# Moving operands of the attention half at 128 bytes past multiples of 256: a hybrid encoder layer on one core

## The chip, the core and the metric

The kernel runs on one core of one Trainium2 chip. The metric is the device time of one execution in microseconds (us). Before the change the median of three runs is 2173.73 us (2172.52 to 2175.91).

## What is computed

One layer of a streaming encoder, on 2048 prompt tokens and 64 sample tokens (2112 in all), width 1024, everything in float32. Cut to what matters:

```python
h = rmsnorm(x, g1) * (1 + sc1) + sh1
proj = h @ w_in                                  # 1024 -> 2568
u, q, k, v, o, gates = jnp.split(proj, cuts, -1)
pool_out = pool_mixer(u, ...)                    # four causal window means, each @ w_pool
hs = mlstm_seq(q, k, v, ig, lf, C, n, m)         # 4 heads of 128, chunks of 64
hs = normed(hs) * sigmoid(o)
x = x + gt1 * (concat([pool_out, hs], -1) @ w_out)
h2 = rmsnorm(x, g2) * (1 + sc2) + sh2
up = h2 @ w_up                                   # 1024 -> 5632
a, g = jnp.split(causal_conv3(up), 2, -1)
x = x + gt2 * ((silu(g) * a) @ w_down)           # 2816 -> 1024
y = rmsnorm(x, g_final)
```

The scales and shifts (sc, sh, gt) come from a conditioning vector through w_ada. The states of the mixers and of the convolution are outputs too.

## The kernel before

**Two halves.** Features lie on the 128 partitions, tokens along the free dimension. The attention half takes the tokens in four groups of 512 (the last one of 576, with the sample tokens), the feed-forward half in three groups of 704. TensorE works through them in a stream: for each group the V projection and the gates (lines 1069 and 1133), per head the projections of q, k and o, then four of u, then eight rows of the output projection. All projections but V go through `gemm` (line 468, its matmul is line 478).

**Three passes.** Every large product is made in float32r from a value split into a high and a low part: a tile has two rows of elements, `[P, 2, n]`, and each block of 128 weights is used three times, high x high, high x low, low x high (`PASSES`, line 463). So each matmul has a stationary operand of 128 x 128 out of a weight tile `wt` and a moving operand out of a tile of the activations:

```python
for pi, (a, b) in enumerate(PASSES):
    for bi, (lo, hi) in enumerate(o.blks):
        pe.matmul(ps[bi][:, :hi - lo], U[:, a, k % 4 * P:(k % 4 + 1) * P], mv[k][:, b, lo:hi],
                  start=(at == 0 and pi == 0), stop=(k == order[-1] and pi == 2))
```

`o.blks` is one block of 512 tokens in the first three groups, and blocks of 256 and 320 in the last. The moving operand `mv` is `hl` (the normed input, `hl_tile`, line 498) for q, k, o and u, and `mx` (the mixers' output, `mx_tile`, line 501) for the output projection. Both are tiles of 2 x 576 float32, 4608 bytes in a partition, so that the low part begins 2304 bytes, nine times 256, behind the high part. In the V projection `hl` is the stationary operand and `wt` moves.

**Weights.** They stream from HBM through SyncE's queue into `raw` buffers (five), and ScalarE and VectorE make high and low parts in `wt` (lines 411 and 414; seven buffers of 4352 bytes, 17 times 256). Weights that come a second time are loaded as split before. `pump` (line 421) keeps some units of work ahead of TensorE.

**Places in the partition.** Pools are stacks: one grows from the left, one from the right (line 93 on). On the left stand `cp` (constants), `wp` (`raw`, `wt`), then `hp` (`hl`), `sm`, `a1` and `a2` (the attention half's small tiles: q, k, th, at, kw, nd, the w4 buffers and others). On the right stand `sp` (scratch), a `gap` of 56 float32 (224 bytes) and `mx`. `half` (line 149) carries 32 float32 of filling, and so does each `wt` (line 175). The attention half's pools are given up before the feed-forward half (`leave`, line 1442), which puts its own tiles there: `hx` on the left, whose operands begin 32 float32 into a tile (`HO = 32`, line 46), and `av` on the right. In the feed-forward half line 1594 (`product`) moves `hx`, lines 2037 and 2160 move `av`; the weights are `wt` in each.

By the build, the operands' places are, in bytes past a multiple of 256:

| operand | where | before |
|---|---|---|
| wt, stationary | all products (moving in V) | 0 (V, 264 columns wide: 0, 32, 64, 96) |
| hl, moving | line 478; stationary in lines 1069, 1133 | 0 |
| mx, moving | line 478 | 0 |
| hx, moving | line 1594 | 128 |
| av, moving | lines 2037, 2160 | 160 or 32 |
| raw, five buffers | lines 411, 414 | 192, 0, 64, 128, 192 |
| q, k, th, at, kw, w4 | heads; line 857's loads | 128 |
| scr, ssum, rb | scratch | 224 |

In the attention half a scheduler orders the instructions of each engine by priority, in the feed-forward half and the first group the order is the program's.

Of the kernel before, what the change touches and what calls it, by code (L numbers as in the profile page):

```python
# [9 lines left out]
F32 = mybir.dt.float32  # L10
# [6 lines left out]
P = 128  # L17
# [47 lines left out]
def tile_layer(ctx: ExitStack, tc: tile.TileContext, xT, vecs, cst, rst, w_mod, w_ada, w_qkou, w_v, w_pool,  # L65
# [25 lines left out]
    rctx, actx = ExitStack(), ExitStack()  # L91
    fctx = ctx.enter_context(ExitStack())
    sp = rctx.enter_context(tc.tile_pool(name="sp", bufs=5, side="right"))
    gap = rctx.enter_context(tc.tile_pool(name="gap", bufs=1, side="right"))
    gap.tile([P, 56], F32, tag="gap", name="gap")
    mx = rctx.enter_context(tc.tile_pool(name="mx", bufs=KD, side="right"))
    hp = actx.enter_context(tc.tile_pool(name="hp", bufs=KD))
    sm = actx.enter_context(tc.tile_pool(name="sm", bufs=2))

# [2214 lines left out]
```

## Time and profile before

| | |
|---|---|
| profiled execution | 2174.68 us |
| its span, first to last instruction | 2172.9 us |
| granted TensorE clock, mean | 0.998 |
| matmuls, weight loads | 13553 each |
| attention half | to about 792 us of the span |
| HBM read, written | 410.98 MB, 125.98 MB |

The page of the profile gives, for each engine, busy time, share of the span and count; matmuls are pipelined, so that one begins while the one before it drains, and the mean duration of one is longer than the time from one start to the next (its period). Groups of instructions are given as line, engine, operation, tiles, size and count, then busy us and mean ns of one, then the idle time ahead of them and what ended it. The timeline merges like instructions in a row: start, length of the whole row, form and count. Waits are given as who waited for whom, total us, times, longest.

### The profile page before, as it was taken

What the parts mean: (1) busy time and instruction counts of PE and PEld (TensorE: products, weight loads), DVE (VectorE), ACT (ScalarE), POOL (GpSimd) and SP (SyncE); (2) the same over time, 40 slices, a digit from 0 to 9 for tenths busy, and PEclk for the clock granted to TensorE, in tenths of its full rate; (3) what the DMA queues carried; (4) which work ended last, traced back from release to release, by engine and by line L of the source; (5) the groups of instructions that cost most, each with busy time, mean ns of one, the idle gap of its engine ahead of it and who ended that gap; (6) DMA issues with size and microseconds to landing.
All of it is one profiled execution on the core that took longest, in us unless ns stands there. A gap on an engine that the chain in (4) does not pass through costs nothing.

```text
span 2172.9 us, 38060 instructions
## 1 busy us (share of the span) xinstructions
PE 2151.4 (99%) x13553; PEld 2044.4 (94%) x13553; DVE 1634.9 (75%) x3040; ACT 1096.1 (50%) x2181; POOL 258.4 (12%) x475
## 2 busy tenths in 40 slices
PE   8999999999999999999999999999999999999998
PEld 7888888888899999999999999999999999999998
DVE  5878668667955778797967668888886597887874
ACT  4554335334333446464736445655655365565554
POOL 0010000001000201010101220100101321111112
PEclk9999999999999999999999999999999999999999
DMA  8987997987888477888967976666668675555542
GB/s 319 328 305 233 323 321 246 309 302 244 301 283 288 169 260 239 282 292 300 350 214 255 321 245 222 234 208 209 228 222 274 223 255 186 170 177 190 171 160 77
DMA packets 297351, 539.51 MB, mean 248 GB/s; under 512 B 25760, under 2 KB 114336, under 8 KB 297160
## 3 DMA queue, kind: packets, MB, share of 16 engines
q1 hardware_dynamic: 286568, 511.87, 69.6%
q10 hardware_dynamic: 10592, 25.20, 3.0%
q8 instruction: 107, 1.75, 0.3%
q14 instruction: 84, 0.69, 0.1%
HBM read 410.98 MB, written 125.98 MB: 247 GB/s over the span
## 4 chain that ended last, share of the span: by engine, by line
PE 85%; DMA 5%; DVE 5%; issue 2%; ACT 2%; SPq 0%; POOL 0%; DVEq 0%; ACTq 0%; POOLq 0%
PE mm L1594 34%; PE mm L478 22%; PE mm L2160 12%; PE mm L2037 8%; PE mm L1133 3%; DVE wt L414 1%; DMA wt<-wsum 1%; PE m L1323 1%; DMA hl_kept<-wt 1%; PE m L1308 1%; PE m L1343 1%; PE m L1345 1%; DVE tg L1572 1%; DMA raw<-w_qkou 0%; ACT wt L411 0%
## 5 line engine op out<-in xcount | busy, mean ns | idle before, releaser
L1594 PE MATMUL mm<-hx,wt 128*128 128x352 f32 x5544 | 885.9, 321 | 0.7 <-DVE wt L414 0.5
L1594 PEld LDWEIGHTS mm<-hx,wt 128*128 128x128 f32 x5544 | 878.7, 188 | 2.6 <-DVE wt L414 2.0
L478 PE MATMUL mm<-hl,wt 128*128 128x512 f32 (+2 forms) x1920 | 387.4, 357 | 0.0
L411 ACT ACTIVATE wt<-raw 128x512 fp32r<-128x512 f32 (+3 forms) x470 | 276.6, 597 | 177.6 <-PE mm L478 52.8
L478 PEld LDWEIGHTS mm<-hl,wt 128*128 128x128 f32 x1920 | 316.4, 189 | 47.7 <-issue 4.4
L414 DVE TENSOR_TENSOR wt<-raw,wt 128x512 fp32r<-128x512 f32 (+3 forms) x470 | 312.8, 672 | 61.9 <-ACT wt L411 61.7
L2160 PE MATMUL mm<-av,wt 128*128 128x448 f32 (+1 forms) x1632 | 262.7, 322 | 0.0
L2160 PEld LDWEIGHTS mm<-av,wt 128*128 128x128 f32 x1632 | 250.4, 188 | 11.1
L2009 DVE SCALAR_TENSOR_TENSOR x<-mm,MOD,x 128x352 f32<-128x352 f32 (+3 forms) x360 | 167.5, 505 | 77.7 <-PE mm L2160 64.3
L2037 PE MATMUL mm<-av,wt 128*128 128x352 f32 x1344 | 220.7, 323 | 1.9 <-DVE x L2009 0.7
L2037 PEld LDWEIGHTS mm<-av,wt 128*128 128x128 f32 x1344 | 215.4, 188 | 5.0 <-DVE ea L1603 3.0
L1641 ACT ACTIVATE mm<-mm 128x352 f32<-128x352 f32 x196 | 87.8, 448 | 233.7 <-PE mm L1594 177.1
L478 PE MATMUL mm<-mx,wt 128*128 128x512 f32 (+1 forms) x960 | 182.9, 352 | 0.3 <-DVE scr L250 0.3
L478 PEld LDWEIGHTS mm<-mx,wt 128*128 128x128 f32 x960 | 159.4, 188 | 23.0 <-PE mm L478 0.5
L1572 DVE SCALAR_TENSOR_TENSOR ta<-ea,V,ta 128x704 f32<-128x704 f32 (+1 forms) x132 | 125.7, 953 | 58.4 <-ACT ta L1567 54.4
L1572 DVE SCALAR_TENSOR_TENSOR tg<-eg,V,tg 128x704 f32<-128x704 f32 (+1 forms) x132 | 125.7, 952 | 56.8 <-ACT tg L1567 54.3
L414 DVE TENSOR_TENSOR wt<-wt 128x512 fp32r<-128x512 f32 x196 | 133.0, 685 | 12.8 <-ACT wt L411 12.7
L411 ACT ACTIVATE wt<-wt 128x512 fp32r<-128x512 f32 x196 | 119.2, 622 | 36.6 <-DMA wt<-wsum 35.7
L1550 POOL COPY ea<-UC 128x2 f32<-128x2 f32 x66 | 33.1, 501 | 506.2 <-DVE ta L1572 407.3
L1781 ACT ACTIVATE tg<-tg 128x704 f32<-128x704 f32 (+1 forms) x66 | 52.5, 795 | 71.8 <-DVE tg L1572 71.8
L1133 PE MATMUL mm<-wt,hl 128*128 128x256 f32 (+1 forms) x576 | 71.4, 284 | 0.0
L1133 PEld LDWEIGHTS mm<-wt,hl 128*128 128x128 f32 x576 | 70.4, 190 | 0.8 <-issue 0.6
(305 smaller groups left out, 2207.0 us busy)
## 6 DMA issues: line engine op xcount, KB each, us to landing
wt<-wsplit SPq DMA_DIRECT2D x132, 512.0 KB, 4.3
raw<-w_up SPq DMA_DIRECT2D x198, 256.0 KB, 3.8
wt<-hl_kept SPq DMA_DIRECT2D x96, 512.0 KB, 6.3
wt<-wsum SPq DMA_DIRECT2D x132, 256.0 KB, 5.0
wsplit<-wt SPq DMA_DIRECT2D x66, 512.0 KB, 5.1
w<-w_up SPq DMA_DIRECT2D x88, 256.0 KB, 4.4
wsum<-w SPq DMA_DIRECT2D x44, 512.0 KB, 5.9
Bd<-fscr ACTq DMA_DIRECT2D x56, 352.0 KB, 4.3
```

Source lines behind the costliest of these rows:

```text
L411: act.activation(u.w[:, 0, :u.n], u.raw[:, :u.n], AF.Copy)
L414: dve.tensor_tensor(out=u.w[:, 1, :u.n], in0=u.raw[:, :u.n], in1=u.w[:, 0, :u.n].bitcast(F32), op=ALU.subtract)
L478: pe.matmul(ps[bi][:, :hi - lo], U[:, a, k % 4 * P:(k % 4 + 1) * P], mv[k][:, b, lo:hi], start=(at == 0 and pi == 0), stop=(k == order[-1] ...
L1133: pe.matmul(ps[ti][:n, :cols], h[4 * kh + k4][:, b, lo:lo + n], U[:, a, k4 % 2 * cols:(k4 % 2 + 1) * cols], start=(kh == 0 and k4 == 0 and ...
L1550: pool.tensor_copy(ext[:, 0:2], UC[:, f, :])
L1572: dve.scalar_tensor_tensor(out=t[:, :E], in0=ext[:, j:j + E], scalar=wc(j, f), in1=t[:, :E], op0=ALU.mult, op1=ALU.add)
L1594: pe.matmul(bk.t[:, :FH], U[:, a, kc * P:(kc + 1) * P], Bo.at(nm, kc, b), start=(first and kc == 0 and pi == 0), stop=(kc == 3 and pi == 2 ...
L1641: act.activation(to.t[:, :FH], bk.t[:, :FH], AF.Copy)
L1781: act.activation(self.tg[:, :E], self.tg[:, :E], AF.Silu)
L2009: dve.scalar_tensor_tensor(out=x3[n][:, a:b], in0=bk.t[:, a - lo:b - lo], scalar=gt2(n, s), in1=x3[n][:, a:b], op0=ALU.mult, op1=ALU.add)
L2037: pe.matmul(bk.t[:, :FH], U[:, a, c:c + P], quad.put(op, m, b), start=(first and m == 0 and pi == 0), stop=(m == 1 and pi == 2), skip_grou ...
L2160: pe.matmul(bks[i].t[:, :hi - lo], U[:, a, k % 4 * P:(k % 4 + 1) * P], av[k][:, b, lo:hi], start=(k == 0 and (a, b) == PASSES[0]), stop=(k ...
```

## The change

```diff
     sp = rctx.enter_context(tc.tile_pool(name="sp", bufs=5, side="right"))
     gap = rctx.enter_context(tc.tile_pool(name="gap", bufs=1, side="right"))
-    gap.tile([P, 56], F32, tag="gap", name="gap")
+    gap.tile([P, 24], F32, tag="gap", name="gap")
     mx = rctx.enter_context(tc.tile_pool(name="mx", bufs=KD, side="right"))
+    actx.enter_context(tc.tile_pool(name="hgap", bufs=1)).tile([P, 32], F32, tag="hgap", name="hgap")
     hp = actx.enter_context(tc.tile_pool(name="hp", bufs=KD))
     sm = actx.enter_context(tc.tile_pool(name="sm", bufs=2))
```

The gap on the right is 128 bytes smaller, so `mx` stands 128 bytes higher. A new unused tile of 128 bytes ahead of `hp` moves `hl` and all that lies behind it on the left by 128 bytes. After it `hl` and `mx` are at 128 past a multiple of 256; q, k, th, at, kw and w4 are on multiples; `wt`, `raw`, `scr` and every tile of the feed-forward half stay. The instructions, their order on each engine and their waits are the same in both programs; line numbers behind the change are one higher.

## The prediction

> **What bounds the kernel now.** I read the head of the page first, then its chain of waits, then the list of what TensorE waited for.
>
> ```profile
> span 2172.9 us, 38060 instructions
> PE 2151.4 (99%) x13553; PEld 2044.4 (94%) x13553; DVE 1634.9 (75%) x3040; ACT 1096.1 (50%) x2181; POOL 258.4 (12%) x475
> PE 85%; DMA 5%; DVE 5%; issue 2%; ACT 2%; SPq 0%; POOL 0%; DVEq 0%; ACTq 0%; POOLq 0%
> PE m L1032 <- DMA mx<-xT: 5.5, 1, 5.5
> PE m L1323 <- DVE kw L250: 1.9, 1, 1.9
> ```
>
> TensorE is busy for 99% of the span, 85% of the chain that ended last is its own, and its longest wait on another engine is 5.5 us at the start, its second longest 1.9 us. So the end is set by the sum of the matmuls' own periods, and a change that lengthens or shortens each of them by a nanosecond shows in full. The next view is busy time in stretches of the attention half (it ends at about 792 us).
>
> ```profile
> 60.00:150.00 90.00, 88.26 (x507) 74.73 (x506) 67.20 (x131) 48.55 (x121) 4.85 (x5) 1.00 0.93 338
> 225.00:380.00 155.00, 155.00 (x832) 131.18 (x831) 117.22 (x241) 62.28 (x149) 10.41 (x15) 1.00 0.87 296
> 560.00:615.00 55.00, 55.00 (x403) 51.99 (x402) 45.60 (x88) 17.11 (x34) 0.00 (x0) 1.00 0.90 300
> 60.00:792.00 732.00, 559.52 (x2836) 467.06 (x2834) 1.00 0.82 279
> ```
>
> The columns are the stretch, its length, busy time and instructions of PE, PEld, DVE, ACT and POOL, the granted clock, the DMA share and GB/s; the last row is the same for line 478 (the projections) alone. TensorE is full in each, at a granted clock of 1.00, so the throttle plays no part. The projections of line 478 are 559.5 of the 732 us: this is what the change can reach. The DMA share is 0.87 to 0.93, high but with no wait behind it.
>
> **The change part by part.** Both programs have the same instructions, waits and order on every engine; only addresses differ. What moves: the moving operands of line 478 (hl and mx, from 0 to 128 past a multiple of 256), hl as the stationary operand of the V projection (lines 1069 and 1133), and by the same 128 bytes all that lies behind hl (q, k, th, at, kw and the w4 buffers come from 128 onto multiples, others from one odd place to another). The weights wt stay on multiples of 256. Nothing is added that could wait; the only thing in question is how fast an unchanged instruction runs.
>
> First, how many there are, with the mean duration of one as the last number before the bar's idle part.
>
> ```profile
> L478 PE MATMUL mm<-hl,wt 128*128 128x512 f32 x1152 | 278.4, 396 | 0.0
> L478 PE MATMUL mm<-mx,wt 128*128 128x512 f32 x576 | 131.3, 389 | 0.0
> L478 PE MATMUL mm<-hl,wt 128*128 128x256 f32 x384 | 105.1, 287 | 0.0
> L478 PE MATMUL mm<-hl,wt 128*128 128x320 f32 x384 | 103.6, 311 | 0.0
> L478 PE MATMUL mm<-mx,wt 128*128 128x320 f32 x192 | 51.4, 312 | 0.3 <-DVE scr L250 0.3
> L478 PE MATMUL mm<-mx,wt 128*128 128x256 f32 x192 | 51.2, 281 | 0.0
> L1594 PE MATMUL mm<-hx,wt 128*128 128x352 f32 x5544 | 885.9, 321 | 0.7 <-DVE wt L414 0.5
> L2037 PE MATMUL mm<-av,wt 128*128 128x352 f32 x1344 | 220.7, 323 | 1.9 <-DVE x L2009 0.7 <-DVE wt L414 0.4 <-DVE ea L1603 0.3
> ```
>
> That is 1152 + 576 = 1728 matmuls of 512 columns and 2 x (384 + 192) = 1152 narrower ones, 2880 in all. Matmuls overlap, so these busy times aren't periods. For a period I take undisturbed stretches of the timeline: (length of the row minus one duration) / (count - 1).
>
> ```profile
> 157.52 11.18 PE L478 MATMUL mm<-hl,wt 128*128 128x512 f32 x48
> 347.02 25.36 PE L478 MATMUL mm<-mx,wt 128*128 128x512 f32 x111
> 766.83 18.45 PE L478 MATMUL mm<-mx,wt 128*128 128x320 f32 x137
> 793.85 11.16 PE L1594 MATMUL mm<-hx,wt 128*128 128x352 f32 x66
> 899.81 47.53 PE L1594 MATMUL mm<-hx,wt 128*128 128x352 f32 x298
> 1039.71 27.09 PE L1594 MATMUL mm<-hx,wt 128*128 128x352 f32 x170
> 1331.03 21.13 PE L2037 MATMUL mm<-av,wt 128*128 128x352 f32 x131
> ```
>
> Periods: hl 512: (11.18 - 0.396)/47 = 229.4 ns; mx 512: 24.97/110 = 227.0; the alternating 256 and 320 columns of the last group: (18.45 - 0.31)/136 = 133.4 for a mean of 288 columns; av 352: 20.81/130 = 160.1; hx 352: 47.21/297 = 159.0 and 26.77/169 = 158.4, but 10.84/65 = 166.8 in the row at 793.85. By the build, mx and hl lie on multiples of 256, av at 160 or 32 past one, hx at 128 past one, wt always on one.
>
> Two rows give a line: (227.0 - 160.1)/(512 - 352) = 0.418 ns a column, and 227.0 - 512 x 0.418 = 13.0 ns for each matmul besides. The third row fits it: 288 x 0.418 + 13.0 = 133.4. So operands at 0, 32 and 160 all pay 13.0 ns. Only hx, at 128, lies below the line, by 1.1 ns (159.0) to 1.7 ns (158.4). This is the one row of the trace in which a moving operand stands 128 bytes past a multiple of 256 against weights on one, which is what the change makes of line 478.
>
> *Term 1.* If the projections get hx's extra time: 2880 x 1.4 ns (the middle) = 4.0 us less; by the two ends 3.2 and 4.9.
> *Term 2.* The hl stretches run 2.4 ns above the mx stretches (229.4 against 227.0) at the same places. They are interrupted more often by the heads' matmuls, and take some time to settle afterwards. Whether the new place settles faster no row shows: between 0 and 1152 x 2.4 ns = 2.8 us; I take 1.0, near the lower end.
> *Term 3.* The V projection, 768 matmuls of 256 or 264 columns by the last four rows below (and a few on 64 weight columns). Here wt moves past hl, which becomes the operand at 128.
>
> ```profile
> 212.56 12.69 PE L1133 MATMUL mm<-wt,hl 128*128 128x264 f32 x103
> 602.38 1.53 PE L1133 MATMUL m<-wt,hl 128*64 128x256 f32 x12
> L1133 PE MATMUL mm<-wt,hl 128*128 128x256 f32 x288 | 36.0, 284 | 0.0
> L1133 PE MATMUL mm<-wt,hl 128*128 128x264 f32 x288 | 35.7, 284 | 0.0
> L1069 PE MATMUL mm<-wt,hl 128*128 128x264 f32 x96 | 14.1, 293 | 0.3 <-ACT hl L994 0.3
> L1069 PE MATMUL p<-wt,hl 128*128 128x256 f32 x96 | 12.1, 282 | 0.0
> ```
>
> Their period is (12.69 - 0.284)/102 = 121.6 ns; the line gives 120.0 for 256 and 123.4 for 264, a mean of 121.7. They sit on the line already, with wt at four different places for the 264. I take 0, with 768 x 1.4 ns = 1.1 us either way.
> *Term 4.* Other engines and DMA. The split of the weights reads its source from raw, whose five buffers stand at 192, 0, 64, 128 and 192 past a multiple of 256, or from wt on one:
>
> ```profile
> L411 ACT ACTIVATE wt<-raw 128x512 fp32r<-128x512 f32 x406 | 251.9, 622 | 139.0 <-PE mm L478 42.9 <-PE mm L2160 31.2 <-PE mm L2037 24.9
> L411 ACT ACTIVATE wt<-wt 128x512 fp32r<-128x512 f32 x196 | 119.2, 622 | 36.6 <-DMA wt<-wsum 35.7 <-DMA wt<-dsum 0.4
> raw<-w_up SPq DMA_DIRECT2D x198, 256.0 KB, 3.8
> wt<-wsum SPq DMA_DIRECT2D x132, 256.0 KB, 5.0
> w<-w_up SPq DMA_DIRECT2D x88, 256.0 KB, 4.4
> ```
>
> ScalarE takes 622 ns from either. A 256 KB load lands in 3.8 us at mixed places (raw), 4.4 at 128 (w) and 5.0 on multiples (wt): the order is not one of alignment. I cost both at nothing. TensorE at 99% hides them; if that cover went, the DMA share of 0.93 in the first group is what would come next, and the stretch 60 to 150 us would then keep none of its gain, about an eighth of term 1 (90 of 732 us), 0.5 us.
>
> Sum: -4.0 - 1.0 = -5.0 us. The profiled execution took 2174.7 us (its span of 2172.9 and 1.8 around it), 1.0 above the median of the runs; -5.0 on the median is 2168.7 us.
>
> A rule speaks against all of this. The Trainium skill, "TensorE: Matmul & The Clock Gate", Part 2, says that PE has two independent SBUF read ports and that loading the next weights takes no bandwidth from the running matmul; its section on the back-to-back gap gives N/2.4 + 2.5 ns. By it 512 columns would take an estimated 215.8 ns, and where the operands lie would not matter. The trace has 227.0 ns, and two periods (166.8 and 159.0) for one shape, so its second sentence does not hold here; the first I keep as a rival.
>
> **The rivals.** *Slower: the new place settles into a longer period.* The row at 793.85 shows 66 matmuls of the same line, shape and places as the 298 at 899.81, at 166.8 ns in place of 159.0: 6.7 ns above the line. So the address alone doesn't set the period; the phase in which a run of matmuls starts picks one of several steady patterns, and at 512 columns the pattern at 128 may be the long one. The hl stretches, 2.4 ns over the mx ones, are a milder form. Price: 1728 x 2.4 = 4.1 us to 1728 x 6.7 = 11.6 us, with the narrow ones as well 2880 x 6.7 = 19.3; its middle, 4.5 ns on 1728, is +7.8, or 2181.5 us. It decides from the point at which the extra time at 128 passes 13.0 ns a matmul. Against it: of 5544 matmuls at 128 only these 66 are shown so slow.
> *No change: 128 past is to the memory as good as on.* av at 160 and 32 differ by just 128 bytes and run in one stretch at one period of 160.1, and 0 fits the same line. For it too that the low period of hx may come from 352 columns and not from its place. It gives 2173.7 us. This is the case in which the skill's first sentence holds.
> *A larger gain.* The lowest fixed part in a row is that of 256 columns on 64 weight columns: (1.53 - 0.277)/11 = 113.9 ns, 6.1 below the line. 2880 x 6.1 = 17.6 us is the far end; half of it gives 2165.
>
> **How the numbers follow.** Forecast (terms 1 and 2; 2166 to 2172): 0.41. Slower pattern (2175 to 2193): 0.32. No change (2173 to 2175): 0.20. Larger gain (2156 to 2166): 0.07. A measurement of this kernel can tell about 0.2% from no change, which is 4.3 us: faster is below 2169.4, slower above 2178.1. Of the forecast about 0.31 lies below 2169.4 and 0.10 above, and of the slower rival 0.03 stays within the bound. Faster 0.38, same 0.33, slower 0.29. The range leaves out the far half of the larger gain and the slow pattern on all 2880 matmuls: 2162 to 2183. The likeliest case's own range is 2166 to 2172.
>
> **What would show it.** In the profile of the changed kernel the undisturbed mx stretch of 512 columns at about 347 us should have a period near 225.5 (forecast), 227.0 (no change) or 230 to 234 (slower); the mean duration of mx 512 should go from 389 to about 387.5, or stay, or rise by as much as the period. The pair rows of the last group should go from 133.4 to about 132. The first L1594 should start about 5 us earlier, and all from there on should be as before, since no operand of the feed-forward half moves; if its own stretches change, a phase that is carried over is at work, and the forecast would be wrong by a mechanism that I priced only for the attention half: a shift of 1 ns there is worth 5.5 us on line 1594 alone.

## The result and the profile after

The changed kernel takes 2179.89 us (median of 12 runs, 2175.75 to 2182.34); the kernel before took 2173.47 us in the same session (12 runs, 2170.73 to 2176.05). The ratio is 1.0028, with a 95% interval of 1.0020 to 1.0036: 4.3 to 7.8 us slower, middle 6.1. The forecast was 5.0 us faster. What came is the first rival, a longer settled period, at about three quarters of its price. The profiled execution took 2181.35 us (span 2179.6).

From the page of the changed kernel: head, chain of waits, and the list of what TensorE waited for. All line numbers are one higher than before.

```profile
span 2179.6 us, 38060 instructions
PE 2158.0 (99%) x13553; PEld 2044.9 (94%) x13553; DVE 1635.6 (75%) x3040; ACT 1095.0 (50%) x2181; POOL 257.7 (12%) x475
PE 89%; DVE 4%; DMA 3%; issue 1%; ACT 1%; SPq 1%; POOL 0%; ACTq 0%; DVEq 0%; POOLq 0%
PE m L1324 <- DVE kw L251: 2.3, 1, 2.3
PE m L1309 <- ACT at L251: 1.8, 1, 1.8
```

The counts are the same, and the added time is TensorE's own: its busy time went from 2151.4 to 2158.0 us (+6.6) for a span that grew by 6.7. VectorE, ScalarE and GpSimd stayed within 1.1 us. Of the waits, that of line 1309 grew most, from 0.5 to 1.8 us; that of line 1230 (1.5 us before) is gone. Next the groups of instructions by form, mean ns of one as the last number before the bar:

```profile
L479 PE MATMUL mm<-hl,wt 128*128 128x512 f32 x1152 | 283.0, 400 | 0.1
L479 PE MATMUL mm<-mx,wt 128*128 128x512 f32 x576 | 134.4, 395 | 0.0
L479 PE MATMUL mm<-hl,wt 128*128 128x320 f32 x384 | 103.2, 308 | 0.0
L479 PE MATMUL mm<-mx,wt 128*128 128x320 f32 x192 | 50.1, 303 | 0.3 <-DVE scr L251 0.3
L1595 PE MATMUL mm<-hx,wt 128*128 128x352 f32 x5544 | 884.9, 321 | 0.1
```

Two signs in one change: 512 columns went up (hl 396 to 400, mx 389 to 395 ns), 320 columns went down (311 to 308, 312 to 303). The feed-forward form of line 1595, which does not move, kept its 321. Periods come from the timeline's stretches, as in the prediction:

```profile
339.78 10.43 PE L479 MATMUL mm<-hl,wt 128*128 128x512 f32 x44
350.51 44.77 PE L479 MATMUL mm<-mx,wt 128*128 128x512 f32 x192
765.82 35.14 PE L479 MATMUL mm<-mx,wt 128*128 128x320 f32 x269
802.87 11.16 PE L1595 MATMUL mm<-hx,wt 128*128 128x352 f32 x66
```

mx 512: (44.77 - 0.395)/191 = 232.3 ns, where it was 227.0. hl 512: (10.43 - 0.400)/43 = 233.3, where a stretch had 229.4. The pairs of the last group: (35.14 - 0.31)/268 = 130.0, where they were 133.4. The last row repeats the odd stretch of 66 feed-forward matmuls to the digit, 11.16 us. In a later execution of the same changed kernel the same 66 matmuls took the short period, (10.61 - 0.321)/65 = 158.3 ns in place of 166.8:

```profile
798.32 10.61 PE L1595 MATMUL mm<-hx,wt 128*128 128x352 f32 x66
```

In the single starts of the trace, mx 512 before is 227, 227, 226 without end; after, it goes round in sevens (for example 228, 229, 233, 240, 234, 230, 232) and never comes to a constant. hl 512 before comes to the same 227, 227, 226, after about nine starts of 225 to 236 ns behind an interruption; in the stretch at 339.78 after, its starts alternate between 229 and 238.

Where the time went, as the length of each phase of the program (from the first matmul of a phase to the first of the next, in us; groups added up). Beside the first profile of each kernel stands the one of its later profiles that has no step, both taken in one session on one chip; "steps" are the drops of the granted clock in the attention half, of which more below.

| execution | V projection | hl 512 | mx 512 | last group, hl | last group, mx | feed-forward | steps | time |
|---|---|---|---|---|---|---|---|---|
| before | 109.97 | 344.52 | 130.78 | 136.33 | 51.70 | 1375.46 | 1 | 2174.68 |
| before, later | 110.52 | 342.85 | 130.78 | 135.55 | 52.07 | 1376.45 | 0 | 2174.50 |
| changed | 109.82 | 348.82 | 133.93 | 138.48 | 51.13 | 1372.88 | 2 | 2181.35 |
| changed, later | 109.54 | 347.63 | 133.95 | 133.58 | 52.82 | 1375.70 | 0 | 2179.33 |

Between the two executions without a step: hl 512 +4.8, mx 512 +3.2, V projection -1.0, last group -2.0 and +0.75, 5.6 us in all to the end of the attention half (with -0.1 at the start). The feed-forward half gives between 1372.9 and 1376.5 us in one or the other, in both directions. What the narrow forms give back also differs between executions of one program: the mx pairs of the changed kernel run at 130.0 ns in three of its four profiles, and in the fourth ("changed, later") at the old (38.52 - 0.31)/286 = 133.6:

```profile
757.89 38.52 PE L479 MATMUL mm<-mx,wt 128*128 128x320 f32 x287 [0.29 <-DVE scr L251]
```

### The profile page after: what moved, and what is told of

It is laid out like the page before. It is cut to its first block, busy times and chain, and to the rows that moved or that the text cites. A ratio compares the mean times of both kernels' runs of the same rounds, so it can differ in the third digit from the quotient of the medians.

```text
span 2179.6 us, 38060 instructions
## 1 busy us (share of the span) xinstructions
PE 2158.0 (99%) x13553; PEld 2044.9 (94%) x13553; DVE 1635.6 (75%) x3040; ACT 1095.0 (50%) x2181; POOL 257.7 (12%) x475
## 4 chain that ended last, share of the span: by engine, by line
PE 89%; DVE 4%; DMA 3%; issue 1%; ACT 1%; SPq 1%; POOL 0%; ACTq 0%; DVEq 0%; POOLq 0%
PE mm L1595 37%; PE mm L479 23%; PE mm L2161 12%; PE mm L2038 8%; PE mm L1134 3%; DVE wt L415 1%; PE m L1324 1%; PE m L1309 1%; PE m L1346 1%; PE m L1344 1%; DMA raw<-w_ada 1%; DVE tg L1573 0%; PE mm L1070 0%; ACT tg L1568 0%; DVE x L2010 0%
## 5 line engine op out<-in xcount | busy, mean ns | idle before, releaser
L479 PE MATMUL mm<-hl,wt 128*128 128x512 f32 (+2 forms) x1920 | 392.0, 360 | 0.1
L415 DVE TENSOR_TENSOR wt<-wt 128x512 fp32r<-128x512 f32 x196 | 133.3, 686 | 10.6 <-ACT wt L412 10.6
```

What stands on the lines that cost most here:

```text
L415: dve.tensor_tensor(out=u.w[:, 1, :u.n], in0=u.raw[:, :u.n], in1=u.w[:, 0, :u.n].bitcast(F32), op=ALU.subtract)
```

## The experiments

**Which tile: hl, mx, or what moved along.** Three variants of the kernel before, each with a part of the change. `agap` is one more unused tile, behind `hp`; with it, 256 bytes in all put the small tiles back on their old residues.

```diff
 hl only:
+    actx.enter_context(tc.tile_pool(name="hgap", bufs=1)).tile([P, 32], F32, tag="hgap", name="hgap")
     hp = actx.enter_context(tc.tile_pool(name="hp", bufs=KD))
+    actx.enter_context(tc.tile_pool(name="agap", bufs=1)).tile([P, 32], F32, tag="agap", name="agap")
 mx only:
-    gap.tile([P, 56], F32, tag="gap", name="gap")
+    gap.tile([P, 24], F32, tag="gap", name="gap")
 small tiles only:
     hp = actx.enter_context(tc.tile_pool(name="hp", bufs=KD))
+    actx.enter_context(tc.tile_pool(name="agap", bufs=1)).tile([P, 32], F32, tag="agap", name="agap")
```

> hl alone stands 128 past a multiple of 256; mx and the small tiles behind hl stay where they were. Theory (the residue of the moving operand against that of the weights sets the period at which a run of matmuls settles): the hl matmuls of 512 columns at about 237 ns as in the changed kernel, mx 512 at 227.0, the hl pairs of 256 and 320 columns about 7 ns a pair shorter than before; 2.5 to 5 us slower than before (2176 to 2179 us). Rival (the tiles that moved along with hl, or their DMAs, are the cause): about 2173.5, with hl 512 at 233.5.

> mx alone stands 128 past a multiple of 256. Theory: mx 512 at 232 in place of 227 ns, 576 x 5 = 2.9 us more, less 192 pairs x 7 ns = 1.3 us; about 1.5 us slower (2175), hl as before. Rival (small tiles): no change and mx 512 at 227.

> hl and mx stay on multiples of 256; only what lies behind hl (q, k, th, at, w4 and so on) moves by 128 bytes as in the changed kernel. Theory: no change (2172.5 to 2174.5), periods as before. Rival (small tiles): slower by up to 6 us.

Measured, against the kernel before on the same chip (2173.08 us): hl only 2175.39, ratio 1.0009 (1.0000 to 1.0018); mx only 2174.52, 1.0006 (0.9998 to 1.0015); small tiles only 2172.13, 0.9994 (0.9986 to 1.0003). The times alone hardly part them, the phases do: mx 512 takes 133.94 us with mx moved and 130.71 and 130.78 in the other two; hl 512 takes 345.82 with hl moved and 342.52 and 342.34 in the other two (no clock step in any of the three). The timeline's mx stretch of the kernel before and of two of them:

before:
```profile
347.02 43.72 PE L478 MATMUL mm<-mx,wt 128*128 128x512 f32 x192
```
mx only:
```profile
347.81 44.77 PE L478 MATMUL mm<-mx,wt 128*128 128x512 f32 x192
```
small tiles only:
```profile
346.61 43.72 PE L479 MATMUL mm<-mx,wt 128*128 128x512 f32 x192
```

With mx alone moved, the stretch has the changed kernel's 44.77 us to the digit. The rival that tiles or DMAs behind hl make the loss falls. "hl only" came out just under what was expected (2175.4 against 2176 to 2179), and the shorter pairs expected of it do not show: its hl part of the last group took 135.88 us, against 135.01 and 135.51 in the other two.

**Against what does the place count?** If the residue of hl and mx by itself mattered, moving the weights would do nothing; if the place relative to the weights matters, moving both restores the old time and moving the weights alone gives the new one. The pad behind an early tile shifts wt by 128 bytes, and with it all that lies behind it on the left: raw, hl and the small tiles. So when all are to move, the unused tile ahead of `hp` falls away and the gap of 24 stays; when wt alone is to move, that tile stands there as in the changed kernel, which brings hl and the small tiles back to their old residues, and the gap is 56 as before.

```diff
-    half = cp.tile([P, 8 + 32], F32, tag="half", name="half")[:, :8]
+    half = cp.tile([P, 8 + 64], F32, tag="half", name="half")[:, :8]
```

> As the changed kernel, with the weights wt moved by 128 bytes as well, so that hl and mx stand at 0 relative to the weights, but at 128 absolutely. If the place relative to the weights decides: hl and mx 512 at 227 to 234 as before, about 2173.5 us for the attention half (the feed-forward half changes too: hx would stand at 128 relative as before, since it moves along). If the absolute residue of the moving operand decides: 232 ns for mx 512 as in the changed kernel, about 2180.

> The weights wt alone move by 128 bytes; hl, mx and the small tiles stay where they were. Theory of the relative place: the projections run as in the changed kernel (mx 512 at 232 ns, pairs at 260), 2176 to 2182 us. Theory of the absolute place of hl and mx: mx 512 at 227.0 as before, 2173.5 us.

The mx stretch with hl, mx and wt all moved:
```profile
346.31 43.72 PE L478 MATMUL mm<-mx,wt 128*128 128x512 f32 x192
```
The same with wt alone moved:
```profile
351.05 44.96 PE L479 MATMUL mm<-mx,wt 128*128 128x512 f32 x192
```

All moved: 43.72 us, as before. Weights alone: 44.96 us, hl 512 at 349.34, the time 2181.45 against 2174.53 us, ratio 1.0035 (1.0024 to 1.0047), although neither hl nor mx was touched (some 2.4 us of it belong to the feed-forward half, as the next paragraph shows). So it is the distance of the moving operand from the stationary one, modulo 256 bytes, that decides, and not an alignment of either. The Trainium skill, "TensorE: Matmul & The Clock Gate", Part 2, has two independent SBUF read ports, one for the streaming operand and one for the weights; these two runs speak against their being independent here.

The kernel with all three moved did not come back to 2173: 2175.95 us, ratio 1.0023 (1.0012 to 1.0033). Its attention half did (hl 512 341.90, mx 512 130.81), but moving wt changes the feed-forward half's distances to av, which stays. By form, before and with all moved:

```profile
L2160 PE MATMUL mm<-av,wt 128*128 128x448 f32 x816 | 178.8, 363 | 0.0
L2160 PE MATMUL mm<-av,wt 128*128 128x256 f32 x816 | 111.0, 280 | 0.0
```
```profile
L2160 PE MATMUL mm<-av,wt 128*128 128x448 f32 x816 | 181.8, 367 | 0.0
L2160 PE MATMUL mm<-av,wt 128*128 128x256 f32 x816 | 110.4, 279 | 0.0
```

The means go from 363 to 367 and from 280 to 279 ns: 816 x (4 - 1) = 2.4 us. Five of its 12 runs lie at 2180.8 to 2184.1 us, apart from the rest; their mean granted clock is 0.997 or 0.998, that of the others 0.997 to 0.999. The profile shows an execution of 2172.83, so what those five had is open.

**TensorE alone.** Next the cost by itself: no other engine and no DMA at work, rows of 72 matmuls with the weights on a multiple of 256 and the moving operand at each of eight places.

```python
    for blks in FORMS:
        for r in PLACES:
            t = [mv[r, k] for k in range(2)]
            for rep in range(2):
                run([small, small], ((0, 132),), 4 + 3 * rep, 0)
                last = run(t, blks, 72 // len(blks), r // 4)
```

> Leaves the computation out: TensorE alone runs unbroken rows of 72 matmuls of one form each (512, 448, 352, 256, 264 columns, and the pairs 256+320 and 288+288), the weights on a multiple of 256 and the moving operand 0, 32, 64 ... 224 bytes past one, each twice from different starting phases; ScalarE, VectorE and the DMA queues stand still meanwhile. Theory (matmul and weight load meet in the memory, and the place of the one against the other sets where a row settles): 512 columns at 0 settle at 226.7 ns, at 128 at 231 to 234; 352 columns at 128 at 158 to 159; the pair 256+320 at 267 for 0 and 260 for 128; the 256 and 264 columns differ by under 2 ns. Rival (the other engines' and the DMAs' traffic make the difference in the kernel): no difference between the places here, all at one line.

Its timeline, the second row of four places (the operand's name has the place in bytes):

```profile
132.68 16.55 PE L100 MATMUL mm<-by0b,wt 128*128 128x512 f32 x72
201.56 16.71 PE L100 MATMUL mm<-by64b,wt 128*128 128x512 f32 x72
270.84 16.95 PE L100 MATMUL mm<-by128b,wt 128*128 128x512 f32 x72
305.67 17.08 PE L100 MATMUL mm<-by160b,wt 128*128 128x512 f32 x72
```

A row has one longer matmul at its start. Without the first six the trace's starts give, for each place in bytes:

| columns | 0 | 32 | 64 | 96 | 128 | 160 | 192 | 224 |
|---|---|---|---|---|---|---|---|---|
| 512 | 226.7 | 233.3 | 228.9 | 233.4 | 232.3 | 234.3 | 233.3 | 233.4 |
| 352 | 160.0, 161.2 | 160.0 | 160.0 | 162.2 | 158.4, 166.7 | 160.0 | 160.0 | 160.1 |
| 256 and 320, mean | 133.1 | 130.9, 131.6 | 131.4 | 133.3 | 133.1 | 132.0 | 131.5 | 133.6 |

(The first row of all, 512 at 0, began at half the clock and is left out of the table.) The kernel's 227.0 and 232.3 ns come back without its traffic, so the rival of the other engines' and the DMAs' share falls. At 512 columns place 0 is the best of the eight; the kernel before stood on it. Where a cell has two numbers, the two starting phases settled differently. The pairs at 128 missed the expectation: 133.1 from both phases here, 130 in the changed kernel. So did the 256 and 264 columns, which were to differ by under 2 ns: they range from 116.7 to 120.0 and from 120.0 to 126.7 by place. And place 0 is not the best for every width: 448 columns take 202.7 ns there and 200.0 at 64.

**The starting phase.** Rows of the same kind, each form eight times behind three matmuls of eight different widths.

> Leaves the computation out, as m_place: rows of 72 matmuls, each form and place eight times, with eight different widths of the three matmuls ahead of it and so eight starting phases. Theory (place, column count and starting phase together pick the settled period): 512 at 0 always at 226.7, 512 at 128 at 232.3 or longer every time, 352 at 128 at 158.4 from some phases and 166.7 from others, 352 at 0 at 160 to 161, pairs at 0 always near 266, at 64 near 263, at 128 at 260, 266 or 271 depending on the phase. Rival (the place alone decides): one period for each form and place.

Four of its 56 rows, 352 columns at 128 and at 0:

```profile
444.10 11.72 PE L101 MATMUL mm<-by0b,wt 128*128 128x352 f32 x72
467.79 11.62 PE L101 MATMUL mm<-by128b,wt 128*128 128x352 f32 x72
479.53 12.20 PE L101 MATMUL mm<-by128b,wt 128*128 128x352 f32 x72
491.85 11.61 PE L101 MATMUL mm<-by128b,wt 128*128 128x352 f32 x72
```

352 at 128 settles at 158.3 to 158.4 ns from six phases and at 166.7 from two; at 0 it is 160.0 from all eight. 512 at 0: 226.7 to 227.0 (one row 228.9, the first, begun at half the clock); 512 at 128: 232.3 to 232.5 from six, 233.4 from two, never less. The pairs: 133.1 at 0 and 131.4 or 131.5 at 64 from all, 129.8 or 133.1 at 128, four times each (271 ns a pair was not seen). The place alone does not set the period; place, column count and the way the row begins do. What was varied is the width of the matmuls ahead; that it acts through the starting phase is the reading of it. In the whole kernel even the same program gives either period, as the two executions of the 66 matmuls above show.

**A better version?** The pairs gain where the 512 columns lose, so the last group alone was moved. hl and mx lie at 64 (or 128), and the first three groups use them from column 48 (or 32) on, which puts their operands back at 0.

```diff
+        o.sh = 0 if o.last else 48
...
-            d = hl_tile(k)
+            d = hl_tile(k)[:, :, o.sh:]
...
-            mix[:NH] = [mx_tile(gi) for gi in range(NH)]
+            mix[:NH] = [mx_tile(gi)[:, :, o.sh:] for gi in range(NH)]
```

> hl and mx lie 64 past a multiple of 256, and the first three groups use them from column 48 on, so that their 512-column operands stand at 0 as before; only the last group's pairs and its V projection stand at 64. By the rows of the kernel in which TensorE ran alone (pairs 131.4 a matmul at 64 against 133.1 at 0, from either starting phase): mx 512 at 227.0 as before, the pairs at 262.8 in place of 267, 576 x 4.2 = 2.4 us less than before, about 2170.5. If the last group then waits longer for the heads' chain on ScalarE and VectorE, part of this is lost.

> The same with the last group at 128 past, as in the changed kernel, and the first three groups at 0 (their column 32 on). If the changed kernel's 260 ns a pair hold: 576 x 7 = 4 us less than before, 2169; if the pairs at 128 settle at 266 to 271, as in the kernel in which TensorE ran alone and in the kernel with the weights moved, no gain to 2 us more.

A third way leaves all addresses and cuts the last group at column 288:

```diff
-        o.blks = [(0, 256), (256, 576)] if o.last else [(0, GT)]
+        o.blks = [(0, 288), (288, 576)] if o.last else [(0, GT)]
```

> Everything lies where it lay before; only the last group is cut at column 288 in place of 256 (two blocks of 288 in place of 256 and 320), so that its second block starts 128 past a multiple of 256 and the first on one. Theory: the pairs lie between 260 ns (both blocks at 128) and 267 (both at 0), so 576 pairs x 0 to 7 ns, 0 to 4 us less than before: 2169.5 to 2173.5. Rival (only the column counts matter): 2 x (288 x 0.418 + 13.0) = 266.8 a pair, no change.

None can be told from the kernel before: at 64, 2174.26 us against 2175.35, ratio 0.9995 (0.9986 to 1.0005); at 128, 2173.96, 0.9998 (0.9989 to 1.0006); cut at 288, 2172.82 against 2174.53, 0.9992 (0.9983 to 1.0002). The last stretch of mx pairs, with the place at 64 and then at 128:

```profile
756.24 38.04 PE L481 MATMUL mm<-mx,wt 128*128 128x320 f32 x287 [0.29 <-DVE scr L252]
```
```profile
752.35 38.52 PE L481 MATMUL mm<-mx,wt 128*128 128x320 f32 x287 [0.29 <-DVE scr L252]
```

The cut at 288 also agrees with TensorE alone, where the two blocks of 288 take 133.2 ns a matmul at place 0, as 256 and 320 do (133.1). At 64 the pairs run nearly as TensorE alone said (131.4), (38.04 - 0.31)/286 = 131.9 a matmul. At 128 they fell into the other pattern, 133.6. With the place at 64 TensorE also stands 1.6 us for line 1311 and 1.1 us once for VectorE's scr:

```profile
PE m L1311 <- ACT at L252: 1.6, 1, 1.6
PE mm L481 <- DVE scr L252: 1.4, 2, 1.1
```

That waiting took the gain is not shown: at the first of the two waits (its line 1308) the unchanged kernel itself stood 0.5, 1.6 and 0.3 us in its three profiles. Nor is it shown that there was no gain, since the interval at 64, from 3.0 us faster to 1.1 slower, holds the 2.4 us expected.

**The clock steps.** The changed kernel's profile shows a granted clock below 1.00 in two places, at the waits of lines 1324 and 1309:

```profile
430.00:450.00 20.00, 17.65 (x90) 14.86 (x89) 11.59 (x27) 4.23 (x11) 1.01 (x1) 0.91 0.92 327
690.00:700.00 10.00, 8.21 (x39) 7.09 (x37) 5.46 (x13) 3.89 (x11) 0.00 (x0) 0.66 1.00 330
```

Whether such a step follows from idle time was asked of TensorE alone: 72 rows of 512 columns at place 0, with nine lengths of idle time between them.

```python
            for _ in range(n):
                dve.tensor_tensor(out=tmp, in0=tmp, in1=tmp, op=ALU.max)
            dve.scalar_tensor_tensor(out=t[0][:, 0, :128], in0=tmp, scalar=0.0, in1=src[:, :128], op0=ALU.mult, op1=ALU.add)
            last = run(t, ((0, 512),), 60 + rep, 0)
```

> Leaves the computation out: TensorE alone runs 72 rows of 60 to 67 matmuls of 512 columns at place 0, and between two rows stands idle for nine different times (about 0.8 to 3.5 us), each eight times, because the next row's operand is written by a chain of VectorE instructions behind the row before. Theory (an idle time of about 2 us makes the clock step down in some executions, which is the part of the changed kernel's loss that varies): no half-clock matmuls (427 ns) after gaps under 1.5 us, after gaps of 1.8 to 2.5 us in some of the eight, after 3 us and more in most; a step costs 2 to 5 us. Rival (the steps in the kernels have another cause): no half-clock matmuls after any gap here, or no relation to its length.

Its timeline, first round (the idle time ahead of a row stands in brackets):

```profile
129.24 13.90 PE L98 MATMUL mm<-by0b,wt 128*128 128x512 f32 x60 [1.03 <-DVE by0b L113]
160.23 13.84 PE L98 MATMUL mm<-by0b,wt 128*128 128x512 f32 x60 [1.78 <-DVE by0b L113]
176.18 15.45 PE L98 MATMUL mm<-by0b,wt 128*128 128x512 f32 x60 [2.10 <-DVE by0b L113]
212.31 16.71 PE L98 MATMUL mm<-by0b,wt 128*128 128x512 f32 x60 [2.76 <-DVE by0b L113]
250.95 13.84 PE L98 MATMUL mm<-by0b,wt 128*128 128x512 f32 x60 [3.42 <-DVE by0b L113]
```

60 matmuls take 13.84 us without a step, 15.45 or 16.71 with one. After idle times of 0.8 to 1.8 us none of 32 rows had one; after 2.1 to 3.4 us 21 of 40 had, and not even 3.4 us brings it every time. A step costs 1.5 to 1.7 us (18 rows, 7 or 8 starts of 427 ns) or 2.7 to 2.9 us (three rows, 13 such starts), where 2 to 5 were expected. The Trainium skill, "TensorE: Matmul & The Clock Gate", Part 1, gives an idle window of about 3.4 us that runs freely and does not begin with the idle time. That one idle time has a step and the next of the same length has none agrees with a free window, and so do the lengths in the traces, where the granted clock holds one value for whole multiples of 3.41 us (430.08, 3.41 and 6.83 in the first profiles of the two kernels). That the idle time has to fill such a window does not agree with the rows, since 2.1 us were enough in three of eight.

The two kernels unedited, profiled again:

> The changed kernel once more, unedited. If the clock steps down after idle times of about 2 us of TensorE make the difference between its runs of 2176 and of 2181, a run near 2176 shows none or one of them and a run near 2181 two; the periods (mx 512 at 232, pairs at 260) are the same in either.

> The changed kernel, unedited, once more profiled. Theory: its time is about 2175.5 to 2177 us without a step of the clock in the attention half, and about 2 us more for each step and the idle time ahead of it (2177 to 2179 with one, 2180 to 2182 with two); mx 512 at 232 ns in any case. Rival: the time does not follow the number of steps.

> The changed kernel, unedited, a further profile. Theory: 2175.5 to 2177 us without a clock step, 2177 to 2179 with one, 2180 to 2182 with two. Rival: the time does not follow the number of steps.

> The kernel before, unedited, once more profiled. Theory: about 2170.5 to 2172.5 us without a step in the attention half, 2173.5 to 2176 with one; mx 512 at 227 ns in any case. Rival: no relation.

> The kernel before, unedited, a further profile. Theory: 2170.5 to 2172.5 us without a clock step, 2173.5 to 2176 with one. Rival: no relation.

The changed kernel: 2179.20 us with one step; then, in the later session, 2187.34 with three and 2179.33 with none. The kernel before in that session: 2177.53 with one, 2174.50 with none. Within the session the order holds, by 3.0 us for one step and 8.0 for three, the longer idle times included. The levels expected fail: without a step both kernels came out 2 us above the upper end, so single executions of different sessions cannot be set side by side to 2 us. In the kernel the wait ahead of a step can be shorter (1.8 us at line 1309) than the shortest that had one here (2.1 us); the narrower matmuls ahead of it end by the trace's model, so the two aren't comparable to 0.3 us. Steps fall on both kernels. They make a part of the scatter and not all of it: of the changed kernel's twelve runs, those of 2175.75 and of 2181.42 us have the same mean granted clock of 0.999, where the profile with two steps has 0.996. Another part is the matmuls that settle either way: counted from the starts in groups of twelve, 132 to 360 of some 5160 matmuls on hx in the seven profiles of the two kernels ran at over 164 ns, at 8.3 ns each 1.1 to 3.0 us. What stays between the two executions without any is 4.8 us.

## Why the prediction was wrong, point by point

- **TensorE's own time sets the end; a nanosecond a matmul shows in full.** Right: +6.6 us busy, +6.7 us span.
- **Same instructions, waits and order; other engines and DMA cost nothing (term 4).** Right: small tiles alone moved, 0.9994 (0.9986 to 1.0003).
- **Term 1, 2880 matmuls x -1.4 ns "if the projections get hx's extra time".** This is the step that failed. The extra time belongs to a place and a column count and a starting phase together. At 352 columns the place 128 may give 158.4; at 512 columns it gives 232.3 or more from every phase, +5.3 ns on mx instead of -1.4. The line through three rows hid it: it took for a fixed cost of 13.0 ns what were three settled patterns. With TensorE alone the line fails already at place 0: it gives 200.3 ns for 448 columns and 123.4 for 264, measured are 202.7 and 120.0. And "operands at 0, 32 and 160 all pay 13.0 ns" holds at 352 columns (160.0 at all three, one row at 0 161.2) and not at 512 (226.7, 233.3, 234.3). No row of line 478 had 512 columns anywhere but at 0, and 0 is the best of the eight.
- **The pairs, 133.4 to about 132.** Right in sign and larger (130.0) in three of the changed kernel's four profiles, but not a property of the place: 133.6 for mx in the fourth and in another build, 129.8 or 133.1 by the phase with TensorE alone.
- **Term 2, hl settles faster, -1.0.** Wrong: before, hl settles at mx's 227.0 ns after some nine matmuls, and the 229.4 was the mean with these; after, mx does not come to a constant, and neither does hl; hl 512 grew by 4.3 us between the first two profiles and by 4.8 between those without a step.
- **Term 3, V projection 0 within 1.1 us.** Held: -0.15 and -1.0 us.
- **The slower rival.** Right in place and price, and in mechanism in part: at 512 columns the long period came from all eight starting phases, so that no phase had to pick it. The price was 4.1 to 11.6 us on the 1728 matmuls of 512 columns, middle 7.8; measured 4.8 + 3.2 = 8.0 between the executions without steps. What the rival left out is what the narrow forms give back in some executions: 2.0 us in hl's part of the last group in this pair, none with hl alone moved. The row at 793.85 was the evidence: read as 66 matmuls of 5544 it seemed rare, while 180 of some 5160 ran so slow in that profile, up to 360 in another, and two of eight phases lead there with TensorE alone.
- **"No change", and the rule of the Trainium skill, "TensorE: Matmul & The Clock Gate", Part 2.** Out: with TensorE alone and nothing else moving, 512 columns take 226.7 to 234.3 ns by place. The formula N/2.4 + 2.5 ns stands there, in "Back-to-back issue gap", for an isolated matmul and not for a stream with a weight load each, so the prediction's 227.0 against 215.8 ns was no proof against the rule; the rows by place are.
- **The first feed-forward matmul about 5 us earlier.** It came 9.0 us later in the first profiles (791.78 to 800.80) and 5.6 us later between those without a step.

Open: why the distance counts. The runs show which distances and beginnings settle where; that the weight load and the moving operand meet in the memory was the theory of the experiment and is not shown. Open too is the share of idle time and clock steps in the 6.1 us: hl only and mx only add up to 3.8 us by the medians, with intervals whose upper ends add up to more than 6, and the pair without steps gives 4.8 us in single executions.

## What to carry to other kernels

A settled period of back-to-back matmuls must not be carried from one column count to another, however well a line fits: put the very form, at the place in question and from several starting phases, into a row of TensorE alone, which takes one run. What counts is the distance between moving and stationary operand, so padding one pool to suit one form changes all forms that use it. Repeat the profile of one program before reading a gain from it: here the same matmuls settled at one period in one execution and at another in the next, and gains of 2 to 4 us in the last group could not be told from the scatter. Idle times of TensorE of over 2 us may cost the clock as well, 1.5 to 2.9 us a time in the rows above.

## What was not expected of the hardware

- Moving only the weights by 128 bytes costs as much as moving hl and mx (mx 512 134.31 against 133.93 us for 576 matmuls); moving all three costs nothing there (130.81).
- With 512 columns at place 0 the row locks at 226.7 ns within ten matmuls, in each of the 51 rows without a clock step in the kernel with idle times.
- One form at one place has two settled periods 8.3 ns apart (352 at 128: 158.4 and 166.7). Which of them a row takes went with the width of the matmuls ahead of it, and in the kernel one row of 66 took either in two executions of the same program (11.16 and 10.61 us).
- After 2.1 us without a matmul the clock may halve for 7 to 13 of the next matmuls of 512 columns (three rows of eight after 2.1 us), and after 3.4 us it may not (two of eight).
